# hi of w1 meets hi and lo of u in one 512-column matmul, the two halves of a PSUM bank added by VectorE

## Chip, core and metric

The kernel runs on one core of a Trainium2 chip. The metric is the device time of one execution in microseconds (us), the median of several runs. Beside it stands one profiled execution, whose trace gives every instruction's engine, start and duration.

## What is computed

Two layers of a decoder trunk on 256 tokens of width 1024, in float32. Each layer adds a token mixer and then a feed-forward part to h:

```python
for i in range(DEPTH):                       # DEPTH = 2
    u = rmsnorm(h, norm_mix[i])
    h = h + mixer_i(u)                       # i = 0: dilated window attention, i = 1: block attention
    h = h + sq_relu_mlp(rmsnorm(h, norm_ffn[i]), ffn_w1[i], ffn_w2[i])

def sq_relu_mlp(h, w1, w2):                  # w1: 1024 x 4096, w2: 4096 x 1024
    return jnp.square(jax.nn.relu(h @ w1)) @ w2
```

The change concerns `h @ w1` and the relu and square behind it.

## The kernel before

**Three matmuls for one product.** To keep float32 accuracy with matmuls that read a shorter type (F32R), each operand is split in two parts: hi, the value rounded to the shorter type, and lo, the rest. A product is then hi x hi + hi x lo + lo x hi, three matmuls that add into the same PSUM region (`mm3`, L228 to L231, and the three lines L652 to L654).

**Splitting.** Weights come from HBM in units of 256 rows by 512 columns (`next_dma`), two slices of 128 rows each. For each slice ScalarE writes hi (L165, L167) and VectorE lo (L175, L177). L167 and L177, the forms with `gt`, also multiply by the gain of the norm; the units of w1 and of the mixers' first products use them, those of w2 don't. Seven units can stand split at once.

**Order.** The program order is written by hand. Every few matmuls the code calls `beat()`: it emits the deferred steps that have come due (`defer(n, step)` means n beats from now), and on every second beat, or when the weights run short, one more slice is split. The order in which steps are emitted is the order in each engine's queue. Each engine works through its queue strictly in that order.

**u.** The normed input is transposed by TensorE (`norm_transpose`, L353). ScalarE copies it out as hi (L360) and VectorE forms lo (L361). u is two pairs of tiles (halves of four k each), one tile for hi and one for lo, 4 x 256 columns each.

**Feed-forward part** (`ffn`, L624). w1 is worked off in eight column blocks j of 512. `up(j)` forms the block's 512 hidden channels as four column blocks c of 128, with the 256 tokens as matmul columns: for each c, and for each of the eight k, three matmuls of 256 columns. `down(j)` multiplies the hidden block by w2 into two pairs of banks, with 512 columns per matmul (L229 to L231, output y). The order is up(0), up(1), down(0), up(2), down(1), and so on. In up(0) each c has a bank of its own, and the loop goes over k = 0 to 3 of all c first, since the second half of u comes later; from j = 1 on two c share one bank. The banks come from the tags "acc", "o", "s" and "tp", two of each, eight in all.

**Eviction.** `relu2` follows when a bank is full: ScalarE applies Relu out of PSUM into r (L636, one beat later), VectorE squares r (L638, three), ScalarE copies it as hi (L639, five), VectorE forms lo (L640, seven). In up(0) that is once per c with 256 columns, from j = 1 on once per two c with 512.

Of the kernel before, what the change touches and what calls it, by code (L numbers as in the profile page):

```python
# [24 lines left out]
F32 = mybir.dt.float32  # L25
F32R = mybir.dt.float32r
AF = mybir.ActivationFunctionType
ALU = mybir.AluOpType
AX = mybir.AxisListType

P = 128
S = 256
# [35 lines left out]
def trunk(ctx, tc, x, rel_bias, norm_mix, norm_ffn, a_w_qkv, a_q_gain, a_k_gain, a_w_o,  # L68
          b_w_qkv, b_q_gain, b_k_gain, b_w_o, ffn_w1, ffn_w2, onehot, mask_a, mask_b, out):
    nc = tc.nc  # L70
# [3 lines left out]
    act = ctx.enter_context(tc.tile_pool(name="act", bufs=1))  # L74
# [6 lines left out]
    def bank(tag, name):  # L81
        return ps.tile([P, 512], F32, tag=tag, bufs=2, name=name)

    def work(tag, bufs, name):
        return act.tile([P, 512], F32, tag=tag, bufs=bufs, name=name)
# [103 lines left out]
    def weight(key, k):  # L189

        i = index[key, k // 2]
        s = 2 * i + k % 2
        st["asked"] = max(st["asked"], s + 1)
        while st["hi"] <= s:
            assert next_hi(), (key, k)
        while st["lo"] <= s:
            next_lo()
        return split[i][0][:, k % 2, :], split[i][1][:, k % 2, :]

    def used(key, k):  # L200
        done.add(index[key, k // 2])
        while st["first"] in done:
            st["first"] += 1

    def defer(beats, fn):
        st["seq"] += 1
        later.append((st["beat"] + beats, st["seq"], fn))

    def beat(n=1):

        for _ in range(n):
            st["beat"] += 1
            while True:
                due = sorted(e for e in later if e[0] <= st["beat"])
                if not due:
                    break
                later.remove(due[0])
                due[0][2]()
            if st["beat"] % 2 == 0 or st["lo"] < st["asked"] + 4:
                next_slice()  # L220
# [7 lines left out]
    def mm3(acc, a, b, first, last):  # L228
        nc.tensor.matmul(acc, lhsT=a[0], rhs=b[0], start=first, stop=False)  # L229
        nc.tensor.matmul(acc, lhsT=a[0], rhs=b[1], start=False, stop=False)  # L230
        nc.tensor.matmul(acc, lhsT=a[1], rhs=b[0], start=False, stop=last)  # L231


    h = const.tile([P, NT, D], F32, name="h")
# [107 lines left out]
    u = {}  # L342
    rstd = {}

    def norm_transpose(which, half, t, natural):

        if t == 0:
            u[half] = tuple(act.tile([P, 4, S], F32R, tag=f"u{half}{s}", bufs=1, name=f"u{s}_{which}_{half}")
                            for s in ("h", "l"))
        tp = bank("tp", f"ut_{which}_{half}_{t}")  # L350
        for c in range(4):
            k = 4 * half + c
            nc.tensor.transpose(out=tp[:, c * P:(c + 1) * P], in_=h[:, t, k * P:(k + 1) * P], identity=ident)  # L353
        hi, lo = u[half]
        i = tp.rearrange("p (c q) -> p c q", c=4)
        if natural:
            hi, lo = (z.rearrange("p c (q t) -> p t c q", t=NT)[:, t] for z in (hi, lo))
        else:
            hi, lo = (z[:, :, t * P:(t + 1) * P] for z in (hi, lo))
        nc.scalar.activation(hi, i, AF.Copy)  # L360
        nc.vector.tensor_sub(lo, i, hi.bitcast(F32))  # L361
# [33 lines left out]
    def norm_half(which, half, natural=False, lead=2):  # L395
        for t in range(NT):
            defer(lead + t, lambda t=t: norm_transpose(which, half, t, natural))
        defer(lead + 3, lambda: norm_squares(which, half))
        if half == 1:
            defer(lead + 7, lambda: norm_scale(which, natural))  # L400

    def ux(k, cols):
        hi, lo = u[k // 4]
        return hi[:, k % 4, cols], lo[:, k % 4, cols]


    V, T, oT = {}, {}, {}
# [213 lines left out]
                nc.vector.scalar_tensor_tensor(hs, acc[t], scale[t], hs, op0=ALU.mult, op1=ALU.add)  # L621


    def ffn(i, after):  # L624
        hid, y = {}, {}

        def up(j):
            key = ("up", i, j)
            hh, hl = hid[j] = tuple(act.tile([P, 4, S], F32R, tag="ol", bufs=4, name=f"h{s}_{i}_{j}") for s in "hl")
            first = j == 0  # L630
            banks = {}

            def relu2(b, c0, n):
                w = n * S
                r = work("z", 3, f"r_{i}_{j}_{b}")[:, :w]
                defer(1, lambda: nc.scalar.activation(r, banks[b][:, :w], AF.Relu))  # L636
                ho, lo = (z[:, c0:c0 + n, :].rearrange("p c q -> p (c q)") for z in (hh, hl))
                defer(3, lambda: nc.vector.tensor_mul(r, r, r))  # L638
                defer(5, lambda: nc.scalar.activation(ho, r, AF.Copy))  # L639
                defer(7, lambda: nc.vector.tensor_sub(lo, r, ho.bitcast(F32)))  # L640

            for c, ks in [(c, r) for r in (range(4), range(4, 8)) for c in range(4)] if first else \
                    [(c, range(8)) for c in range(4)]:
                b, off = (c, 0) if first else (c // 2, c % 2 * S)
                if b not in banks:
                    banks[b] = bank("acc" if b < 2 else "o", f"up_{i}_{j}_{b}")
                o = banks[b][:, off:off + S]
                for k in ks:
                    whi, wlo = weight(key, k)
                    uh, ul = ux(k, slice(0, S))  # L650
                    cols = slice(c * P, (c + 1) * P)
                    nc.tensor.matmul(o, lhsT=whi[:, cols], rhs=uh, start=k == 0, stop=False)  # L652
                    nc.tensor.matmul(o, lhsT=whi[:, cols], rhs=ul, start=False, stop=False)  # L653
                    nc.tensor.matmul(o, lhsT=wlo[:, cols], rhs=uh, start=False, stop=k == 7)  # L654
                    if c == 3 and k % 2:
                        used(key, k)
                    if k % 2:
                        beat()
                if ks[-1] == 7 and first:
                    relu2(b, c, 1)  # L660
                elif ks[-1] == 7 and c % 2:
                    relu2(b, c - 1, 2)

        def down(j):
            hh, hl = hid[j]
            for n in range(2):
                key = ("down", i, j, n)
                if j == 0:
                    y[n] = [bank("so"[n], f"y_{i}_{n}_{t}") for t in range(NT)]
                tail = i == 1 and j == 7 and n == 1  # L670
                for k, t in [(k, t) for t in range(NT) for k in range(4)] if tail else \
                        [(k, t) for k in range(4) for t in range(NT)]:
                        q = slice(t * P, (t + 1) * P)
                        mm3(y[n][t], (hh[:, k, q], hl[:, k, q]), weight(key, k), j == 0 and k == 0, j == 7 and k == 3)
                        if t == 1 and k % 2:
                            used(key, k)
                        beat()
                if j == 7:
                    after(n, y[n])

        up(0)
        for j in range(8):
            if j < 7:
                up(j + 1)
            down(j)


    for t in range(NT):
        norm_transpose(0, 0, t, False)
        keep_warm(1)  # L690
        for _ in range(2):
            next_hi()
            next_lo()
    for t in range(NT):
        defer(4 + t, lambda t=t: norm_transpose(0, 1, t, False))
# [24 lines left out]
    acc = {0: [bank("acc", f"wo_a_0_{t}") for t in range(NT)]}  # L720
# [11 lines left out]
    def to_second(n, y):  # L732
        add_half(n, y, rstd)
        norm_half(2, n, natural=True, lead=3)

    ffn(0, to_second)
    place("b", lambda m: 48 + 8 * m if m < 4 else (81.5, 87.5, 94, 100.5)[m - 4],
          lambda m: 57 + 8 * m if m < 4 else 90 + 6 * (m - 4),
          lambda m: (82, 82, 88, 88, 101, 101, 113, 113)[m])
    project("b", order_b)  # L740
    acc = {0: [bank("acc", f"wo_b_0_{t}") for t in range(NT)]}
# [12 lines left out]
    def to_out(n, y):  # L754
        for t in range(NT):
            for i in range(2 if n == 1 and t == 1 else 1):
# [4 lines left out]
                (nc.scalar if i else nc.sync).dma_start(ov[:, t, c0:c0 + w], hs)  # L761

    ffn(1, to_out)
    flush()

# [26 lines left out]
```

## Time and profile before

| | |
|---|---|
| median of 3 runs | 634.81 us (634.78 to 634.92) |
| profiled execution | 634.84 us, its span 633.0 us |
| TensorE busy, matmuls | 627.3 us, 3902 instructions |
| VectorE busy | 427.1 us |
| ScalarE busy | 385.2 us |
| moved by DMA | 113.62 MB, mean 180 GB/s |

The span runs from the first to the last instruction. Busy times are unions of the instructions' durations. A matmul's duration is modelled and matmuls overlap, so what one of them costs is read from the distance of starts. Engine names in the rows: PE is TensorE, PEld its weight loads, DVE is VectorE, ACT is ScalarE, POOL is GpSimd.

### The profile page before, as it was taken

The numbers are of one execution on the slowest core, as the hardware profiler recorded it, in microseconds if no ns is written. First come the engines' busy times: TensorE is split into PE (matmuls) and PEld (weight loads), VectorE is DVE, ScalarE is ACT, GpSimd is POOL, SyncE is SP. The second block draws the span as 40 slices with busy tenths as digits, with TensorE's granted clock in tenths as the row PEclk, the third lists the DMA queues.
The fourth block names the chain that finished last, engine by engine and source line by source line (L and its number), as shares of the span: only waits on it lengthen the run. The fifth ranks groups of instructions, "written<-read, shape, count | busy, mean of one in ns | idle before, by whom it ended". The sixth has DMA issues, their size and how long they took to land.

```text
span 633.0 us, 10380 instructions
## 1 busy us (share of the span) xinstructions
PE 627.3 (99%) x3902; PEld 545.7 (86%) x3902; DVE 427.1 (67%) x767; ACT 385.2 (61%) x742; POOL 36.6 (6%) x23
## 2 busy tenths in 40 slices
PE   8999999999999999999999999999999999999997
PEld 7778887888989989998988877877999899899886
DVE  5877989766875466467547789887776744754651
ACT  6976876675765356346437778786765643653540
POOL 1222230000000000000000322000000000000000
PEclk9999999999999999999999999999999999999999
DMA  7986456423654564574556666463467446635701
GB/s 247 320 217 211 129 196 173 152 100 134 226 174 169 199 227 139 187 246 140 176 179 198 195 186 195 135 195 134 142 207 251 150 160 223 218 130 187 249 17 67
DMA packets 74538, 113.62 MB, mean 180 GB/s; under 512 B 4584, under 2 KB 30504, under 8 KB 74488
## 3 DMA queue, kind: packets, MB, share of 16 engines
q1 hardware_dynamic: 74312, 112.82, 54.6%
q8 instruction: 31, 0.51, 0.3%
q14 instruction: 19, 0.16, 0.1%
q10 hardware_dynamic: 176, 0.14, 0.1%
HBM read 111.81 MB, written 1.13 MB: 178 GB/s over the span
## 4 chain that ended last, share of the span: by engine, by line
PE 98%; DMA 1%; ACT 0%; DVE 0%; issue 0%; DVEq 0%; SPq 0%; ACTq 0%
PE up L654 10%; PE up L653 10%; PE up L652 10%; PE y L230 9%; PE y L229 9%; PE y L231 9%; PE acc_a L229 6%; PE acc_a L230 5%; PE acc_a L231 5%; PE acc_b L229 4%; PE acc_b L231 3%; PE acc_b L230 3%; PE s_a L518 1%; PE o_a L583 1%; PE ut L353 1%; PE wo_b L229 1%
## 5 line engine op out<-in xcount | busy, mean ns | idle before, releaser
L177 DVE SCALAR_TENSOR_TENSOR lo<-raw,gt,hi 128x512 fp32r<-128x512 f32 x248 | 174.5, 745 | 6.9 <-ACT hi L167 6.8
L167 ACT ACTIVATE hi<-raw,gt 128x512 fp32r<-128x512 f32 x248 | 162.9, 713 | 5.0 <-DMA raw<-in_a_w_qkv_dram 2.0
L652 PE MATMUL up<-uh,hi 128*128 128x256 f32 x512 | 145.1, 283 | 0.0
L654 PE MATMUL up<-uh,lo 128*128 128x256 f32 x512 | 144.9, 283 | 0.0
L653 PE MATMUL up<-ul,hi 128*128 128x256 f32 x512 | 144.9, 283 | 0.0
L175 DVE TENSOR_TENSOR lo<-raw,hi 128x512 fp32r<-128x512 f32 x152 | 98.3, 686 | 43.7 <-ACT hi L165 43.3
L165 ACT ACTIVATE hi<-raw 128x512 fp32r<-128x512 f32 x152 | 88.1, 624 | 54.1 <-PE up L653 21.4
L229 PE MATMUL y<-hi,hh 128*128 128x512 f32 x256 | 100.0, 390 | 0.0
L230 PE MATMUL y<-lo,hh 128*128 128x512 f32 x256 | 99.8, 390 | 0.0
L231 PE MATMUL y<-hi,hl 128*128 128x512 f32 x256 | 99.6, 389 | 0.0
L652 PEld LDWEIGHTS up<-uh,hi 128*128 128x128 f32 x512 | 98.2, 192 | 0.6
L653 PEld LDWEIGHTS up<-ul,hi 128*128 128x128 f32 x512 | 98.2, 192 | 0.5
L654 PEld LDWEIGHTS up<-uh,lo 128*128 128x128 f32 x512 | 98.2, 192 | 0.0
L638 DVE TENSOR_TENSOR r<-r 128x512 f32<-128x512 f32 (+1 forms) x36 | 22.7, 631 | 68.5 <-ACT r L636 68.5
L636 ACT ACTIVATE r<-up 128x512 f32<-128x512 f32 (+1 forms) x36 | 19.8, 550 | 76.1 <-PE up L654 75.7
L229 PE MATMUL acc_a<-hi,uh 128*128 128x512 f32 x144 | 60.3, 419 | 0.0
L231 PEld LDWEIGHTS y<-hi,hl 128*128 128x128 f32 x256 | 48.1, 188 | 10.1
L231 PE MATMUL acc_a<-hi,ul 128*128 128x512 f32 x144 | 56.7, 394 | 0.0
L230 PE MATMUL acc_a<-lo,uh 128*128 128x512 f32 x144 | 56.6, 393 | 0.0
L229 PEld LDWEIGHTS y<-hi,hh 128*128 128x128 f32 x256 | 48.1, 188 | 9.6
L230 PEld LDWEIGHTS y<-lo,hh 128*128 128x128 f32 x256 | 48.1, 188 | 9.4
L229 PE MATMUL acc_b<-hi,uh 128*128 128x512 f32 x96 | 40.0, 417 | 0.0
(128 smaller groups left out, 776.6 us busy)
## 6 DMA issues: line engine op xcount, KB each, us to landing
raw<-in_ffn_w_dram SPq DMA_DIRECT2D x128, 512.0 KB, 4.8
raw<-in_a_w_qkv_dram SPq DMA_DIRECT2D x64, 256.0 KB, 4.0
raw<-in_b_w_qkv_dram SPq DMA_DIRECT2D x24, 512.0 KB, 4.5
raw<-in_b_w_o_dram SPq DMA_DIRECT2D x8, 512.0 KB, 4.8
bias_a<-vdram_a SPq DMA_DIRECT2D x20, 128.0 KB, 5.6
raw<-in_a_w_qkv_dram SPq DMA_DIRECT2D x4, 512.0 KB, 6.3
raw<-in_a_w_o_dram SPq DMA_DIRECT2D x4, 512.0 KB
bias_b<-vdram_b SPq DMA_DIRECT2D x8, 256.0 KB, 4.6
```

Source lines behind the costliest of these rows:

```text
L165: nc.scalar.activation(hi, w, AF.Copy)
L167: nc.scalar.activation(hi, w, AF.Copy, scale=gt[:, gain + c:gain + c + 1])
L175: nc.vector.tensor_sub(lo, w, hi.bitcast(F32))
L177: nc.vector.scalar_tensor_tensor(lo, w, gt[:, gain + c:gain + c + 1], hi.bitcast(F32), op0=ALU.mult, op1=ALU.subtract)
L229: nc.tensor.matmul(acc, lhsT=a[0], rhs=b[0], start=first, stop=False)
L230: nc.tensor.matmul(acc, lhsT=a[0], rhs=b[1], start=False, stop=False)
L231: nc.tensor.matmul(acc, lhsT=a[1], rhs=b[0], start=False, stop=last)
L636: defer(1, lambda: nc.scalar.activation(r, banks[b][:, :w], AF.Relu))
L638: defer(3, lambda: nc.vector.tensor_mul(r, r, r))
L652: nc.tensor.matmul(o, lhsT=whi[:, cols], rhs=uh, start=k == 0, stop=False)
L653: nc.tensor.matmul(o, lhsT=whi[:, cols], rhs=ul, start=False, stop=False)
L654: nc.tensor.matmul(o, lhsT=wlo[:, cols], rhs=uh, start=False, stop=k == 7)
```

## The change

hi and lo of u become two planes of one tile per half, [128, 4, 2, 256], so that for each k the 256 columns of hi and the 256 of lo lie side by side. Hi of w1 then meets both in one matmul of 512 columns into a whole bank: the first half of the bank collects hi x hi, the second hi x lo. Lo of w1 meets hi of u in a matmul of 256 columns into the first half. For k = 7 the narrow matmul comes first, so that the last one covers the whole bank. Each c has a bank of its own in every up; from j = 1 on the third and fourth come from the tag "tp". VectorE adds the two halves of each bank with a `tensor_reduce` that writes 256 numbers; relu and square become one `scalar_tensor_tensor`, r = max(r, 0) x r. The steps behind are due at beats 1, 2, 4 and 6 where it was 1, 3, 5 and 7. Everything else stays.

```diff
@@ norm_transpose
-            u[half] = tuple(act.tile([P, 4, S], F32R, tag=f"u{half}{s}", bufs=1, name=f"u{s}_{which}_{half}")
-                            for s in ("h", "l"))
+            u[half] = act.tile([P, 4, 2, S], F32R, tag=f"u{half}", bufs=1, name=f"u_{which}_{half}")
...
-        hi, lo = u[half]
+        hi, lo = (u[half][:, :, s, :] for s in range(2))
@@ ux
-        hi, lo = u[k // 4]
-        return hi[:, k % 4, cols], lo[:, k % 4, cols]
+        return tuple(u[k // 4][:, k % 4, s, cols] for s in range(2))
@@ ffn, up
-            def relu2(b, c0, n):
+            def relu2(c0, n):
                 w = n * S
-                r = work("z", 3, f"r_{i}_{j}_{b}")[:, :w]
-                defer(1, lambda: nc.scalar.activation(r, banks[b][:, :w], AF.Relu))
+                r = work("z", 3, f"r_{i}_{j}_{c0}")[:, :w]
+                for c in range(c0, c0 + n):
+                    defer(1, lambda c=c: nc.vector.tensor_reduce(
+                        r[:, (c - c0) * S:(c - c0 + 1) * S], banks[c].rearrange("p (s q) -> p q s", s=2), op=ALU.add, axis=AX.X))
                 ho, lo = (z[:, c0:c0 + n, :].rearrange("p c q -> p (c q)") for z in (hh, hl))
-                defer(3, lambda: nc.vector.tensor_mul(r, r, r))
-                defer(5, lambda: nc.scalar.activation(ho, r, AF.Copy))
-                defer(7, lambda: nc.vector.tensor_sub(lo, r, ho.bitcast(F32)))
+                defer(2, lambda: nc.vector.scalar_tensor_tensor(r, r, 0.0, r, op0=ALU.max, op1=ALU.mult))
+                defer(4, lambda: nc.scalar.activation(ho, r, AF.Copy))
+                defer(6, lambda: nc.vector.tensor_sub(lo, r, ho.bitcast(F32)))
...
-                b, off = (c, 0) if first else (c // 2, c % 2 * S)
-                if b not in banks:
-                    banks[b] = bank("acc" if b < 2 else "o", f"up_{i}_{j}_{b}")
-                o = banks[b][:, off:off + S]
+                if c not in banks:
+                    banks[c] = bank("acc" if c < 2 else "o" if first else "tp", f"up_{i}_{j}_{c}")
                 for k in ks:
                     whi, wlo = weight(key, k)
-                    uh, ul = ux(k, slice(0, S))
+                    both = u[k // 4][:, k % 4].rearrange("p s q -> p (s q)")
                     cols = slice(c * P, (c + 1) * P)
-                    nc.tensor.matmul(o, lhsT=whi[:, cols], rhs=uh, start=k == 0, stop=False)
-                    nc.tensor.matmul(o, lhsT=whi[:, cols], rhs=ul, start=False, stop=False)
-                    nc.tensor.matmul(o, lhsT=wlo[:, cols], rhs=uh, start=False, stop=k == 7)
+                    if k < 7:
+                        nc.tensor.matmul(banks[c], lhsT=whi[:, cols], rhs=both, start=k == 0, stop=False)
+                    nc.tensor.matmul(banks[c][:, 0:S], lhsT=wlo[:, cols], rhs=both[:, 0:S], start=False, stop=False)
+                    if k == 7:
+                        nc.tensor.matmul(banks[c], lhsT=whi[:, cols], rhs=both, start=False, stop=True)
```

## Rows read from the trace of the kernel before

**Rows 1.** The page: engines' busy time, share, instructions; granted clock in 40 slices.
```profile
PE 627.3 (99%) x3902; PEld 545.7 (86%) x3902; DVE 427.1 (67%) x767; ACT 385.2 (61%) x742; POOL 36.6 (6%) x23
...
PEclk9999999999999999999999999999999999999999
```
**Rows 2.** The page: chain of waits that ended last, by engine and by line.
```profile
PE 98%; DMA 1%; ACT 0%; DVE 0%; issue 0%; DVEq 0%; SPq 0%; ACTq 0%
PE up L654 10%; PE up L653 10%; PE up L652 10%; PE y L230 9%; PE y L229 9%; PE y L231 9%; PE acc_a L229 6%; PE acc_a L230 5%; PE acc_a L231 5%; PE acc_b L229 4%; PE acc_b L231 3%; PE acc_b L230 3%; PE s_a L518 1%; PE o_a L583 1%; PE ut L353 1%; PE wo_b L229 1%
```
**Rows 3.** Timeline, 250 to 262 us: start, duration, engine, line, operation, operands, count.
```profile
250.41 0.39 PE L229 MATMUL y<-hi,hh 128*128 128x512 f32 x1
...
254.49 0.39 PE L229 MATMUL y<-hi,hh 128*128 128x512 f32 x1
...
255.17 0.28 PE L652 MATMUL up<-uh,hi 128*128 128x256 f32 x1
...
255.40 0.28 PE L654 MATMUL up<-uh,lo 128*128 128x256 f32 x1
...
255.52 0.28 PE L652 MATMUL up<-uh,hi 128*128 128x256 f32 x1
```
**Rows 4.** Timeline of TensorE, 262 to 268 us: the end of that up.
```profile
266.32 0.28 PE L652 MATMUL up<-uh,hi 128*128 128x256 f32 x1
...
266.68 0.40 PE L229 MATMUL y<-hi,hh 128*128 128x512 f32 x1
...
267.15 0.39 PE L231 MATMUL y<-hi,hl 128*128 128x512 f32 x1
...
267.84 0.39 PE L231 MATMUL y<-hi,hl 128*128 128x512 f32 x1
```
**Rows 5.** Instructions by line and shape: count, busy us, mean ns, idle before.
```profile
L177 DVE SCALAR_TENSOR_TENSOR lo<-raw,gt,hi 128x512 fp32r<-128x512 f32 x248 | 174.5, 745 | 6.9 <-ACT hi L167 6.8
...
L638 DVE TENSOR_TENSOR r<-r 128x512 f32<-128x512 f32 x28 | 19.4, 692 | 68.5 <-ACT r L636 68.5
...
L636 ACT ACTIVATE r<-up 128x512 f32<-128x512 f32 x28 | 16.7, 598 | 74.4 <-PE up L654 74.4
...
L537 DVE TENSOR_REDUCE nmax_a<-L_a 128x1 f32<-128x512 f32 x16 | 11.0, 686 | 0.6
L535 DVE TENSOR_TENSOR L_a<-s_a,bias_a 128x512 f32<-128x512 f32 x16 | 10.9, 683 | 1.7 <-PE s_a L518 1.6
```
**Rows 6.** Busy time by stretch: one up, one down.
```profile
255.00:266.60 11.60, 11.60 (x98) 11.56 (x97) 3.96 (x6) 3.53 (x6) 0.00 (x0) 1.00 0.49 180
266.60:277.50 10.90, 10.90 (x51) 9.04 (x50) 9.12 (x15) 8.22 (x14) 0.00 (x0) 1.00 0.56 186
```
**Rows 7.** Timeline of VectorE, 230 to 278 us: after an up.
```profile
267.51 0.69 DVE L638 TENSOR_TENSOR r<-r 128x512 f32<-128x512 f32 x1 [0.90 <-ACT r L636]
...
270.06 4.06 DVE L177 SCALAR_TENSOR_TENSOR lo<-raw,gt,hi 128x512 fp32r<-128x512 f32 x6
```
**Rows 8.** Timeline of VectorE, 140 to 186 us: first up of layer 0.
```profile
161.27 1.41 DVE L177 SCALAR_TENSOR_TENSOR lo<-raw,gt,hi 128x512 fp32r<-128x512 f32 x2
162.60 0.41 DVE L638 TENSOR_TENSOR r<-r 128x256 f32<-128x256 f32 x1
162.94 0.74 DVE L177 SCALAR_TENSOR_TENSOR lo<-raw,gt,hi 128x512 fp32r<-128x512 f32 x1
...
163.93 0.74 DVE L177 SCALAR_TENSOR_TENSOR lo<-raw,gt,hi 128x512 fp32r<-128x512 f32 x1
164.60 0.42 DVE L640 TENSOR_TENSOR hl<-r,hh 128x256 fp32r<-128x256 f32 x1
...
165.27 0.68 DVE L175 TENSOR_TENSOR lo<-raw,hi 128x512 fp32r<-128x512 f32 x1
```
**Rows 9.** Timeline of TensorE, 148 to 180 us: the second up starts.
```profile
165.48 0.28 PE L652 MATMUL up<-uh,hi 128*128 128x256 f32 x1
```

More of the change, by code (lines that the diff above doesn't have):

```diff
@@ L659, in up @@
                 if ks[-1] == 7 and first:
-                    relu2(b, c, 1)
+                    relu2(c, 1)
                 elif ks[-1] == 7 and c % 2:
-                    relu2(b, c - 1, 2)
+                    relu2(c - 1, 2)
         def down(j):
```

## The prediction, made before the changed kernel ran

> **What bounds the kernel now.** I read the engine totals first, then the chain of waits, then the matmuls one by one, and only then the other engines. TensorE has work in 627.3 of 633.0 us, its granted clock is full in every slice, and VectorE and ScalarE are busy for 67% and 61% [rows 1]. Busy TensorE alone proves little, because matmuls are pipelined. The chain of waits decides: 98% of it is TensorE, and the three matmul lines of the first feed-forward product, L652 to L654, hold 10% each [rows 2]. So whatever shortens TensorE's own sequence there shortens the kernel, as long as no other engine then comes late.
>
> How long a matmul really occupies TensorE is the distance from its start to the next start, not the duration printed beside it. In the down product (512 columns) L229 starts at 250.41 and again at 254.49 with 18 matmuls between: 4.08 / 18 = 0.2267 us each [rows 3]. In the up product (256 columns) L652 starts at 255.52 [rows 3] and, 30 groups of three later, at 266.32 [rows 4]: 10.80 / 90 = 0.1200 us each. Doubling the columns adds 0.1067 us, which is what 256 columns take at one per cycle of the 2.4 GHz level that the full clock stands for. Of either size, 0.0133 us remains that does not depend on the columns. Each matmul instruction pays it once.
>
> **The change, part by part.**
>
> *Matmuls.* A group is the work of one slice of w1 (k) on one column block (c): before, three matmuls of 256 columns, 3 x 0.1200 = 0.3600 us. After, one of 512 and one of 256 columns: 0.2267 + 0.1200 = 0.3467 us. The columns are the same 768; one fixed part goes. There are 2 layers x 8 j x 4 c x 8 k = 512 groups: 512 x 0.0133 = 6.8 us less. The weight load that goes with the removed matmul goes too; the remaining loads stand as before under the matmul ahead of them: the load for the wide one under a 256-column one, as now in every group, and the other under a longer one. That k = 7 takes lo before hi changes only the order.
>
> What the trace does not show is the two sizes alternating. It shows the changes of size. From up to down, the first two wide matmuls after the change take 0.235 us each (266.68 to 267.15) and the first five 0.232 (to 267.84), then it is 0.2267 [rows 4]. From down to up, the first two narrow ones take 0.115 (255.17 to 255.40), then it is 0.12 [rows 3]. Bounds of a group: at best 0.2267 + 0.115 = 0.3417, a saving of 512 x 0.0183 = 9.4 us; at worst 0.235 + 0.120 = 0.355, a saving of 2.6 us. In an alternation every matmul is the first after a change, so both deviations should come together, 0.232 + 0.115 = 0.347. That is the steady sum again, and I take 0.3467.
>
> The Trainium skill, page "TensorE: Matmul & The Clock Gate", section "Back-to-back issue gap", speaks against this size: an isolated warm matmul costs its columns plus 2.5 ns, so that dropping 512 of them would give 512 x 0.0025 = 1.3 us and 633.5 us. Both spacings of this trace exceed that formula by about 11 ns, and the measurement decides; a rival below keeps what is left of the rule.
>
> *Eviction.* Before, ScalarE reads a bank with Relu (L636, 0.60 us for 512 columns) and VectorE squares (L638, 0.69). After, VectorE adds the two halves of each bank with a reduce, one per c, 64 in all, and the relu and the square are one scalar_tensor_tensor. ScalarE loses its 36 Relus (28 of them on 512 columns, 16.7 us [rows 5]), which lay off the path. The reduce reads 512 numbers of a bank, in pairs 256 apart, and writes 256. No such row exists. The nearest: a reduce of 512 numbers to one, L537, 686 ns, and an add of 512 numbers out of PSUM, L535, 683 ns [rows 5]; I take 0.69 us. Bounds: 0.41 us if it ran at the pace of 256 results (L638 on 256 columns, [rows 8]), and 0.69 + (0.69 - 0.41) = 0.97 us if each result cost another step. The scalar_tensor_tensor I price like L177, 745 ns for 512 against 692 for the square [rows 5]. VectorE gains 64 x 0.69 + 36 x 0.05 = 46 us and stands at 473 of 626 us, by which it is not the bound on the mean.
>
> *Steady periods.* A period is one up and one down, 7 per layer. VectorE is busy 3.96 us of the 11.6 us of up and 9.12 us of the 10.9 us of down [rows 6]; it gains 4 x 0.69 + 2 x 0.05 = 2.9 us, 16.0 of 22.1. The burst that matters comes after an up: the square at 267.51 after 0.90 us of idle time, then the splits of w1's next block, the last six from 270.06 to 274.12 [rows 7]. The reduce of c = 2 fits into that idle time, because its bank is complete a quarter of an up earlier. The reduce of c = 3 takes the place of the Relu that VectorE waited for. So the burst moves back by 0.7 us at most (one reduce, the dearer square) to 274.8, and the next up starts 10.9 us after the last one's end at 266.6 [rows 6], at 277.5. Cost nothing; the cover is those 2.7 us. PSUM: from j = 1 on, an up holds four banks, two of the tag "acc" and two of "tp"; their reduces run at the latest just after that up, and the next up starts 10.9 us later. Cost nothing.
>
> *The first up of each layer.* Here VectorE has hardly a gap, no down lies between this up and the next, and the next up takes all eight slices of its w1 block within its first column block. In VectorE's queue the last of these splits (the last L177 ahead of the first L175) starts at 163.93 and ends at 164.67 [rows 8]. The second up starts at 165.48 [rows 9] and wants the slice for k = 7 after seven groups. In the new order three reduces come ahead of that split, and of the shorter chain one more square and the first subtraction of hl: operations follow each other some 0.08 us sooner than their durations say (two splits of 0.74 take 1.33, from 161.27 to 162.60 [rows 8]), so 3 x 0.61 + 3 x 0.05 + 0.34 + 0.34 = 2.66 us, and the split ends at 167.33. The up starts 32 x 0.0133 = 0.43 us sooner, at 165.05; the slice is wanted at 165.05 + 7 x 0.347 = 167.48, its load 0.12 us before that, at 167.36. There is no margin left. I take 0.1 us of waiting in each layer, 0.2 us; with reduces of 0.97 us it is 3 x 0.28 + 0.1 = 0.9 us in each, 1.9 us; with 0.41 us, none. TensorE waits behind the weight load alone; the rest of that up has its weights by then.
>
> *One tile for u.* hi and lo of u become two planes of one tile, so that the second half of hi (ScalarE) may have to wait for the first half of lo (VectorE), where today they are separate tiles. Taken as nothing, since TensorE has other matmuls to run during the norms; at most a part of one VectorE operation of 0.69 us, which would reach the first up as lateness and lies within its bound above.
>
> *Sum.* The profiled execution has 634.84 us, 633.0 of them span and 1.8 around it; it lies 0.03 us over the median, so that no correction is needed. 634.84 - 6.8 + 0.2 = 628.2 us.
>
> **The rivals.**
>
> *Alternating sizes eat most of the saving.* If every wide matmul behaves like the first two after a change and no narrow one gives anything back, a group takes 0.355 us: 634.84 - 2.6 + 0.2 = 632.4 us. For it: all five wide starts after an up are long. Against it: the narrow ones after a wide one are short by nearly as much.
>
> *A strained first up.* Reduces of 0.97 us and the full wait: 634.84 - 6.8 + 1.9 = 629.9 us. For it: the missing margin. Against it: both nearest rows say 0.69.
>
> *VectorE becomes the bound, and the kernel is slower.* Place: its queue in the first two ups of each layer, later every period. Each 0.1 us more per reduce costs 3 x 0.1 x 2 = 0.6 us in the first ups, so 6.6 us are gone when a reduce takes 0.69 + 1.1 = 1.8 us. In the periods VectorE's own work fills 22.0 us when four reduces take 22.0 - 13.2 = 8.8 us, 2.2 us each. At three times the row, 2.07 us, the first ups lose 3 x 1.38 x 2 + 0.2 = 8.5 us: 636.5 us. For it: stepping through a bank in pairs is nowhere in the trace. Against it: none of the operations on 512 numbers in [rows 5] takes over 0.75 us.
>
> *The product hardly gets shorter.* If the fixed 0.0133 us came not with each instruction but with each 256 columns of this type, the wide matmul would cost two narrow ones, a group would stay at 0.36 us, and the time at 634.8; if a fifth of it goes with the instruction, 1.4 us, it is 633.6 with the wait in the first ups. Against it: the down product has the same type and the double width at 0.2267, not 0.24. The skill's formula above, which knows only 2.5 ns per instruction, would end here.
>
> **How the numbers follow.** The forecast, 628.2, with its ends at 625.4 (groups of 0.3417, no wait) and 629, has 0.66; the strained first up, 629.9, 0.11; the alternation, 632.4, 0.11; the product hardly shorter, 633.6 to 634.8, 0.05; VectorE as the bound, 636.5, 0.07. The range goes from 625.4 to 632.4, the bounds of the group with those of the first ups inside; it leaves out the last two cases and a part of the alternation. A measurement of this kernel tells 0.2%, 1.3 us, from no change: faster means below 633.5. Forecast, strained first up and nearly all of the alternation are: 0.87. Within 0.2%: 0.06. Slower: 0.07.
>
> **What would show it.** Right: starts of the wide and narrow matmul that add up to 0.347 us; an up of 11.1 us where it was 11.5; reduces near 0.69 us; TensorE still nearly all of the chain. Wrong: pairs of 0.355 us; or waits of the weight load for lo in the second up of each layer well over 0.1 us; or reduces above 1 us, with VectorE in the chain during the periods.

## The result: 631.04 us, 3.8 us less

The changed kernel takes 631.04 us (median of 4 runs, 630.81 to 631.7) against 634.87 us; the ratio is 0.994, with a 95% interval of 0.9923 to 0.9958. Beside the version of the last experiment, on another chip, it was 0.9936 (0.9924 to 0.9949). The forecast was 628.2: direction and range hold, but only 3.8 of the expected 6.6 us came.

The page of the changed kernel, engines first, then the chain that ended last by engine and line, answers to [rows 1, 2]:

```profile
PE 622.7 (99%) x3390; PEld 518.0 (82%) x3390; DVE 468.5 (74%) x831; ACT 368.0 (58%) x706; POOL 36.6 (6%) x23
...
PE 96%; DVE 1%; DMA 1%; ACT 1%; issue 0%; SPq 0%; DVEq 0%; ACTq 0%
PE up L652 17%; PE up L653 10%; PE y L229 9%; PE y L231 9%; PE y L230 9%; PE acc_a L229 6%; PE acc_a L230 5%; PE acc_a L231 5%; PE acc_b L229 3%; PE acc_b L231 3%; PE acc_b L230 3%; PE up L655 2%; PE s_a L516 1%; PE o_a L581 1%; PE wo_b L229 1%; PE pt_a L559 1%
```

TensorE has 512 matmuls fewer (3902 to 3390) and still makes up nearly the whole chain. VectorE went from 427.1 to 468.5 us and does not stand in the chain for more than 1%. So the missing gain lies inside TensorE's own sequence. One up from its first matmul to the first of the down behind it, then the start of the next up, in the timeline of TensorE (start, duration, ...):

```profile
232.34 0.39 PE L652 MATMUL up<-u,hi 128*128 128x512 f32 x1
232.56 0.28 PE L653 MATMUL up<-u,lo 128*128 128x256 f32 x1
232.68 0.40 PE L652 MATMUL up<-u,hi 128*128 128x512 f32 x1
...
243.61 0.40 PE L229 MATMUL y<-hi,hh 128*128 128x512 f32 x1
...
254.50 0.39 PE L652 MATMUL up<-u,hi 128*128 128x512 f32 x1
```

243.61 - 232.34 = 11.27 us, 0.3522 us per group, where [rows 3, 4] gave 266.68 - 255.17 = 11.51 and the forecast wanted 0.3467 per group, 11.09 for the up. All steady ups agree to 0.01 us. Over them a wide matmul starts 0.235 us before the next one and a narrow one 0.117, where each in a stream of its own takes 0.2267 and 0.1200. An up and its down together, from the start of one up to the start of the next, take 254.50 - 232.34 = 22.16 us; the kernel before took 22.42 (255.17 to 277.59).

The new work of VectorE, by line and shape (count, busy us, mean ns, idle before):

```profile
L636 DVE TENSOR_REDUCE r<-up 128x256 f32<-128x512 f32 x64 | 43.7, 688 | 37.7 <-PE up L655 37.6
...
L639 DVE SCALAR_TENSOR_TENSOR r<-r 128x512 f32<-128x512 f32 x28 | 19.4, 692 | 1.0
```

The start of the profiled run differs from that of the kernel before. Two stretches of it, busy time by engine and granted clock:

```profile
5.00:8.00 3.00, 1.21 (x9) 0.92 (x7) 0.93 (x2) 1.54 (x3) 0.00 (x0) 0.97 0.90 297
8.00:15.00 7.00, 7.00 (x28) 5.34 (x29) 5.88 (x10) 6.09 (x11) 0.00 (x0) 0.77 0.87 309
```

TensorE worked 1.21 of the 3 us before 8 us, and then was granted 0.77 of its clock, a mean between its two levels of 1.2 and 2.4 GHz; before, it had worked 2.27 of the same 3 us and had the full clock throughout. What decides is not shown: in the run of the order called runs of two below it had worked 1.42 of these 3 us and kept the full clock. At the first up this run is 0.6 us later than the profile of before (153.70 against 153.11). Other runs of the same kernel have 0.999 and 1.0 of the clock over the whole span and take 0.4 us less, and the same kernel in its second profile has the full clock from 8 to 15 us and starts the first up at 152.93. So the late start belongs to the run, not to the change.

### The profile page after: what moved, and what is told of

It reads as the page before. It is cut to its first block, busy times and chain, and to the rows that moved or that the text cites. A ratio compares the mean times of both kernels' runs of the same rounds, so it can differ in the third digit from the quotient of the medians.

```text
span 629.4 us, 9371 instructions
## 1 busy us (share of the span) xinstructions
PE 622.7 (99%) x3390; PEld 518.0 (82%) x3390; DVE 468.5 (74%) x831; ACT 368.0 (58%) x706; POOL 36.6 (6%) x23
## 3 DMA queue, kind: packets, MB, share of 16 engines
HBM read 111.81 MB, written 1.13 MB: 179 GB/s over the span
## 4 chain that ended last, share of the span: by engine, by line
PE 96%; DVE 1%; DMA 1%; ACT 1%; issue 0%; SPq 0%; DVEq 0%; ACTq 0%
PE up L652 17%; PE up L653 10%; PE y L229 9%; PE y L231 9%; PE y L230 9%; PE acc_a L229 6%; PE acc_a L230 5%; PE acc_a L231 5%; PE acc_b L229 3%; PE acc_b L231 3%; PE acc_b L230 3%; PE up L655 2%; PE s_a L516 1%; PE o_a L581 1%; PE wo_b L229 1%; PE pt_a L559 1%
## 5 line engine op out<-in xcount | busy, mean ns | idle before, releaser
L177 DVE SCALAR_TENSOR_TENSOR lo<-raw,gt,hi 128x512 fp32r<-128x512 f32 x248 | 174.6, 744 | 7.4 <-ACT hi L167 7.3
L652 PE MATMUL up<-u,hi 128*128 128x512 f32 x448 | 161.1, 398 | 0.0
L653 PE MATMUL up<-u,lo 128*128 128x256 f32 x512 | 133.3, 281 | 0.0
L653 PEld LDWEIGHTS up<-u,lo 128*128 128x128 f32 x512 | 96.6, 189 | 5.9
L652 PEld LDWEIGHTS up<-u,hi 128*128 128x128 f32 x448 | 84.3, 188 | 17.8
L640 ACT ACTIVATE hh<-r 128x512 fp32r<-128x512 f32 (+1 forms) x36 | 21.1, 585 | 104.1 <-DVE r L639 104.1
L636 DVE TENSOR_REDUCE r<-up 128x256 f32<-128x512 f32 x64 | 43.7, 688 | 37.7 <-PE up L655 37.6
L229 PE MATMUL acc_a<-hi,u 128*128 128x512 f32 x144 | 60.6, 421 | 0.5 <-ACT hi L167 0.5
L231 PE MATMUL acc_a<-hi,u 128*128 128x512 f32 x144 | 57.0, 396 | 0.0
L230 PE MATMUL acc_a<-lo,u 128*128 128x512 f32 x144 | 56.9, 395 | 0.0
L229 PE MATMUL acc_b<-hi,u 128*128 128x512 f32 x96 | 40.0, 417 | 0.0
L231 PE MATMUL acc_b<-hi,u 128*128 128x512 f32 x96 | 37.6, 392 | 0.0
L230 PE MATMUL acc_b<-lo,u 128*128 128x512 f32 x96 | 37.5, 391 | 0.0
```

The lines of the kernel that those rows point to most:

```text
L177: nc.vector.scalar_tensor_tensor(lo, w, gt[:, gain + c:gain + c + 1], hi.bitcast(F32), op0=ALU.mult, op1=ALU.subtract)
L636: defer(1, lambda c=c: nc.vector.tensor_reduce(r[:, (c - c0) * S:(c - c0 + 1) * S], banks[c].rearrange("p (s q) -> p q s", s=2), op=ALU.ad ...
L640: defer(4, lambda: nc.scalar.activation(ho, r, AF.Copy))
L652: nc.tensor.matmul(banks[c], lhsT=whi[:, cols], rhs=both, start=k == 0, stop=False)
L653: nc.tensor.matmul(banks[c][:, 0:S], lhsT=wlo[:, cols], rhs=both[:, 0:S], start=False, stop=False)
```

## The experiments

Theory 1: matmuls of unlike width one behind the other take longer than their steady times add up to; each change of width costs. Theory 2: the wide matmul takes 0.235 us in this place, whatever is beside it (its operands, its bank, VectorE's reads of the neighbouring bank). Theory 3: the weight load for the wide matmul only just fits under 256 columns. Theory 4: the new eviction holds TensorE up.

**Runs of eight.** Only the order of the matmuls changes: per column block wide for k = 0 to 6, all eight narrow ones, wide for k = 7.

```diff
-                for k in ks:
-                    (wide, narrow; for k = 7 narrow, wide)
+                ops = [("w", k) for k in ks if k < 7] + [("n", k) for k in ks] + [("w", k) for k in ks if k == 7]
+                for m, (kind, k) in enumerate(ops):
+                    (that one matmul; a beat after every fourth)
```

> Per column block the wide matmuls of k = 0 to 6 stand together, then the eight narrow ones, then the wide one of k = 7: two changes of width per eight groups where there were sixteen; the same matmuls, nothing else. An up takes 11.27 us in the changed kernel, 32 groups of 0.352. Theory 1, each change of width costs about 3.3 ns: an up of 32 x 0.3467 + 4 x 0.0067 = 11.12 us, and 16 x 0.15 = 2.4 us less in all, near 628.5 us. Theory 2, the wide matmul costs 0.236 us here whatever stands beside it (operands, bank, VectorE's reads): 11.27 us as before, 631.0 us.

Its timeline, runs of like matmuls merged:

```profile
231.59 1.75 PE L655 MATMUL up<-u,hi 128*128 128x512 f32 x7
...
242.74 0.40 PE L229 MATMUL y<-hi,hh 128*128 128x512 f32 x1
...
253.64 1.07 PE L655 MATMUL up<-u,hi 128*128 128x512 f32 x4
```

11.15 us, and 629.6 us in all (629.27 to 631.26); the ratio to before is 0.9907 (0.989 to 0.9923). The same matmuls on the same operands and banks, with the same eviction, are 0.12 us faster per up when like stands beside like, and 0.11 us over up and down (22.05 against 22.16). Theory 2 falls, and with it the part of theory 4 that would slow every matmul. Theory 1 had put 11.12 us and 628.5 us: right in kind, its price of a change too small.

The kernel before shows the same delay where bank, weights and moving operand are others: its first five wide matmuls behind an up's narrow ones take 1.16 us [rows 4], and the first five wide ones behind the narrow ones inside this up take 1.16 us too, where five steady ones take 1.13.

**All 512 columns.**

```diff
-nc.tensor.matmul(banks[c][:, 0:S], lhsT=wlo[:, cols], rhs=both[:, 0:S], start=False, stop=False)
+nc.tensor.matmul(banks[c], lhsT=wlo[:, cols], rhs=both, start=False, stop=False)
```

> The narrow matmul is widened to 512 columns (lo of w1 meets hi and lo of u, a fourth product is added), so that no width changes inside an up, while operands, banks and VectorE's work stay. Theory 1: all matmuls at the steady 0.2267 us, an up of 64 x 0.2267 = 14.51 us, near 683 us in all. Theory 2: a wide matmul on u at 0.236 us, 64 x 0.2358 = 15.09 us, near 692 us.

```profile
244.88 0.39 PE L652 MATMUL up<-u,hi 128*128 128x512 f32 x1
...
259.38 0.39 PE L229 MATMUL y<-hi,hh 128*128 128x512 f32 x1
```

14.50 us for 64 matmuls, 0.2266 each; 682.63 us in all. With one width the wide matmuls on u have their steady time, in the same place with the same weights; an up and its down take 25.39 us, which is 112 x 0.2267. This speaks against theory 2 once more.

**512 and 384 columns.**

```diff
+nc.tensor.matmul(banks[c][:, 0:384], lhsT=wlo[:, cols], rhs=both[:, 0:384], start=False, stop=False)
```

> The narrow matmul is widened to 384 columns (half of the fourth product is added): the width still changes with every matmul, but a weight load has half as many columns more to hide under. Theory 1 (any change of width): 0.2267 + 0.1733 + 0.0067 = 0.4067 us per group, an up of 13.01 us, near 659 us. Theory 3, the load for the wide matmul only just fits under 256 columns and spoils the rhythm: 0.4000 us, 12.80 us, near 655.5 us. Theory 2: 0.4091 us, 13.09 us.

```profile
239.27 0.39 PE L652 MATMUL up<-u,hi 128*128 128x512 f32 x1
...
252.41 0.40 PE L229 MATMUL y<-hi,hh 128*128 128x512 f32 x1
```

13.14 us, 0.4106 per group; 661.06 us. With more room for the weight load the excess did not vanish, as theory 3 wanted; it grew, from 0.0055 us per group to 0.0106 over the steady sum of 0.2267 + 0.1733. The second of these is an estimate, halfway between the two widths; no run shows 384 columns alone, so the size of the growth is not shown. Theory 1 had forecast 13.01: right in kind, too small. Theory 3 falls by this, and by the kernel before, where every load goes under a 256-column matmul and the steady distance is 0.1200 all the same.

**Narrow matmuls, new eviction.** For k = 1 to 6 the wide matmul is split into its halves again.

```diff
+                    elif k < 7:
+                        nc.tensor.matmul(banks[c][:, 0:S], lhsT=whi[:, cols], rhs=both[:, 0:S], start=False, stop=False)
+                        nc.tensor.matmul(banks[c][:, S:], lhsT=whi[:, cols], rhs=both[:, S:], start=False, stop=False)
```

> The wide matmul of k = 1 to 6 is split into its two halves of 256 columns again; the eviction by VectorE, the banks and the one tile for u stay as in the changed kernel. 24 of 32 groups are three narrow matmuls. If the new eviction, banks or tile slow TensorE's matmuls, a narrow one takes more than 0.120 us; if not (theory 1), an up takes 24 x 0.3600 + 8 x 0.3533 = 11.47 us, and the whole 631.0 + 16 x 0.20 = 634.2 us.

```profile
233.65 0.39 PE L652 MATMUL up<-u,hi 128*128 128x512 f32 x1
...
245.04 0.40 PE L229 MATMUL y<-hi,hh 128*128 128x512 f32 x1
```

11.39 us; 634.15 us in all. Eviction, banks and the common tile do not lengthen a narrow matmul. The up is even 0.02 us under the steady sum (24 x 0.36 + 8 x 0.3467 = 11.41); the down behind it loses as much, for up and down take 22.29 us (the next up starts at 255.94), exactly the steady sum (80 x 0.12 + 56 x 0.2267). Where two wide ones stand among twenty or so narrow ones, the narrow ones give back what the wide ones take. So a change of width has no fixed price.

**The matmuls alone.** ScalarE's Relu reads the first half of each bank, as it did before; the sum of the second half is left out.

```diff
-                    defer(1, lambda c=c: nc.vector.tensor_reduce(...))
+                    defer(1, lambda c=c: nc.scalar.activation(r[:, (c - c0) * S:(c - c0 + 1) * S], banks[c][:, 0:S], AF.Relu))
```

> The matmuls, banks and tile of the changed kernel with the old eviction: ScalarE's Relu reads the first half of each bank, VectorE squares as before; the add of the second half (hi of w1 on lo of u) is left out of the result. VectorE loses its 64 reduces, 43.7 us. If the reduces are hidden everywhere: an up of 11.27 us and 631.0 us, as in the changed kernel. If they hold TensorE up, by bank or by lateness, ups get shorter: towards 11.10 us each and 628.3 us.

```profile
232.64 0.39 PE L651 MATMUL up<-u,hi 128*128 128x512 f32 x1
...
243.91 0.40 PE L229 MATMUL y<-hi,hh 128*128 128x512 f32 x1
```

11.27 us again, 23.43 and 23.41 for the first two ups of the layers together as in the changed kernel (23.43 and 23.41), 631.52 us in all in a run whose clock at the start was low (0.997 over the span). The 43.7 us of reduces are hidden everywhere. Theory 4 falls.

**Runs of two, runs of four.** How the excess depends on the number of changes. The loop of the first experiment goes over pieces of two or four k.

> Two wide matmuls, then two narrow ones: 8 changes of width per column block, against 14 in the changed kernel (k = 7 and k = 0 of the next block are both wide, k = 6 and 7 narrow side by side) and 2 in runs of eight. Without any cost of changes an up is 32 x 0.3467 = 11.09 us; the changed kernel has 0.177 us more over 56 changes, 3.2 ns each; the runs of eight 0.06 us over 8, 7.5 ns each. If a change costs a fixed 3.2 ns: 11.20 us. If a change upsets the matmuls behind it until some five of a kind have run, so that it costs more the longer the run: near 11.25 us, hardly better than alternating. In all 630 to 631 us.

> Four wide, then four narrow: 4 changes per column block, 16 per up. A fixed 3.2 ns per change: 11.14 us. A cost that grows with the run, about 7 ns at this length: 11.20 us. In all 629 to 630.5 us.

```profile
231.52 0.62 PE L655 MATMUL up<-u,hi 128*128 128x512 f32 x2
...
242.75 0.40 PE L229 MATMUL y<-hi,hh 128*128 128x512 f32 x1
```

```profile
231.50 1.07 PE L655 MATMUL up<-u,hi 128*128 128x512 f32 x4
...
242.68 0.40 PE L229 MATMUL y<-hi,hh 128*128 128x512 f32 x1
```

| order, 32 wide and 32 narrow | changes per up | up, us | over 11.09 | up and down, us | over 21.97 | per change |
|---|---|---|---|---|---|---|
| alternating (changed kernel) | 56 | 11.27 | 0.18 | 22.16 | 0.19 | 3.3 ns |
| runs of two | 32 | 11.23 | 0.14 | 22.13 | 0.15 | 5 ns |
| runs of four | 16 | 11.18 | 0.09 | 22.07 | 0.09 | 6 ns |
| runs of eight | 8 | 11.15 | 0.06 | 22.05 | 0.08 | 10 ns |

(The count: for k = 7 the narrow one comes first, so two narrow ones meet inside a column block and two wide ones at its border; alternating has 14 changes per block, not the 16 of the first expectation.) The price per change is worked out from up and down together, with a steady sum of 32 x 0.3467 + 48 x 0.2267 = 21.97 us, because part of what the last change of an up costs falls into the down: the up alone would give 7 ns for runs of eight. The kernel before, with two changes in an up and its down, has 22.42 us where its steady sum is 22.40, again 10 ns per change. The fewer the changes, the shorter the up, in every step. A fixed price is refuted, since it would have given 11.20 and 11.14; a price that grows with the run had been put at 11.25 and 11.20. Both measured values lie between. In all 631.91 us and 629.34 us, one run each; the first is above its forecast because 3.7 us of it lie outside the span of 628.2 us, where about 2 are usual. Why is not shown.

**Each reduce twice.**

```diff
-                for c in range(c0, c0 + n):
+                for c in [c for c in range(c0, c0 + n) for _ in range(2)]:
```

> Each reduce is issued twice, so VectorE has 64 more of 0.69 us. In the first up of each layer three more come ahead of the split that the second up wants for k = 7: it ends 3 x 0.61 = 1.8 us later. In the changed kernel it ends at 167.93 us and is wanted near 168.2, so the margin is 0.3 us and TensorE should wait 1.5 us per layer in the second up: 634 us, all other ups 11.27 us. If the steady periods have no room either, their ups get longer as well, by up to 1.2 us each, towards 650 us. If nothing is late: 631.0 us.

In the second up of layer 0 the split for k = 7 (timeline of VectorE) and the narrow matmuls for k = 6 and 7 (of TensorE):

```profile
169.43 0.74 DVE L177 SCALAR_TENSOR_TENSOR lo<-raw,gt,hi 128x512 fp32r<-128x512 f32 x1
```

```profile
168.28 0.28 PE L653 MATMUL up<-u,lo 128*128 128x256 f32 x1
170.23 0.38 PE L653 MATMUL up<-u,lo 128*128 128x256 f32 x1 [1.68 <-DVE lo L177]
```

The waits of TensorE list the same line twice, once per layer:

```profile
PE up L653 <- DVE lo L177: 3.4, 2, 1.7
```

The matmul for k = 7 starts 1.95 us after its neighbour instead of 0.12, 1.83 us lost, and the first two ups of a layer take 25.30 us instead of 23.43. The expectation had 1.5: a doubled reduce starts 0.72 us behind its twin and not 0.61, three of them are 2.16 us, and the margin of 0.27 us is all that covers it. All other ups keep their 11.27. The place that the prediction named is the only one that gives. In all 636.22 us against an expected 634: the span is 633.3 us, 3.9 more than in the profile of the changed kernel, of which 2 x 1.87 are the loss in the first two ups; the other 2.9 us lie outside the span, where that profile had 1.8.

**The two versions side by side.**

> The changed kernel once more, beside the next one on the same chip, so that both are compared with the same runs of the kernel before. Ups of 11.27 us; 3.8 to 4.0 us less than before, a ratio near 0.994.

> The runs of eight once more. Its ups of 11.15 us are 0.117 us shorter than those of the changed kernel, twelve of them, and 0.2 us in the first two ups of each layer: 12 x 0.117 + 2 x 0.2 = 1.8 us less, a ratio near 0.991. If the order of the matmuls were no cause, both would have the same time.

Against the same runs of the kernel before: the changed kernel 630.85 us, 0.9936 (0.9924 to 0.9949); runs of eight 629.62 us, 0.9909 (0.9894 to 0.9924). Ups of 11.27 and 11.15 us as before. The medians are 1.2 us apart where up and down explain 1.7 (12 x 0.107 + 2 x 0.2). The runs of one kernel scatter by more than that gap, 630.75 to 632.7 and 628.95 to 630.14, but the two ranges do not touch: the version with runs beats both others.

## Why the prediction was right or wrong

**The bound.** Right: TensorE's sequence sets the end before and after, and what was saved there came out in the time: 512 x (0.3600 - 0.3522) = 4.0 us, with 3.8 measured.

**The fixed part of a matmul.** Right, as far as one width goes: 0.2266 us in an up of 512-column matmuls only, the value of the down product in [rows 3]. The formula of the Trainium skill ("TensorE: Matmul & The Clock Gate", section "Back-to-back issue gap"), which the page gives for an isolated matmul, would have 0.2158 with its 2.5 ns per instruction. No run here shows that, and the measurement decides.

**The step that failed** is the one behind "in an alternation every matmul is the first after a change, so both deviations should come together, 0.232 + 0.115 = 0.347". Both came, but not with equal weight: wide ones 0.235, narrow ones 0.117, together 0.3522. The term was mis-sized by 512 x 0.0055 = 2.8 us. 628.2 + 2.8, less the 0.2 of waiting that did not come, is 630.8, and that is what the runs of the changed kernel with nearly the full clock took (630.81 and 630.84). The bounds were right (0.3417 to 0.355); the fault was to take the sum of two transients, each read off a single place (0.115 is half of 0.23 us, printed to 0.01), as a proof that they cancel. The steady value had no more standing than the two ends, and the middle of the bounds, 0.3484, would have been no better founded but nearer. The rival with the alternation had the mechanism, at 632.4 as its end; the truth lies between it and the forecast, nearer to the rival.

**The eviction.** Right: 688 ns for the reduce against 0.69 taken, 468.5 us of VectorE against 473. The scalar_tensor_tensor took 692 ns and not 745: it costs what the square did, and the dearer L177, which also reads a factor for each partition, was the wrong neighbour. No consequence.

**Steady periods.** Right, and the cover is there: doubling all reduces left them at 11.27.

**One tile for u.** Right, nothing is to be seen: in the first up of layer 0 the first eight groups take 3.60 us to the start of the ninth (153.70 to 157.30), before 3.66 (153.11 to 156.77).

**The first up of each layer.** The place was right, and the time of the split was right. The rows of the changed kernel (VectorE, then TensorE), which answer to [rows 8, 9]:

```profile
167.19 0.74 DVE L177 SCALAR_TENSOR_TENSOR lo<-raw,gt,hi 128x512 fp32r<-128x512 f32 x1
```

```profile
167.97 0.40 PE L652 MATMUL up<-u,hi 128*128 128x512 f32 x1
168.20 0.40 PE L653 MATMUL up<-u,lo 128*128 128x256 f32 x2
168.44 0.40 PE L655 MATMUL up<-u,hi 128*128 128x512 f32 x1
```

The split ends at 167.93; less the 0.6 us by which this run is later from its start, that is 167.35, and the forecast was 167.33. Its matmul is the second of the two at 168.20, whose load goes under the first: a margin of 0.27 us where none was expected. The slower pairs made most of it, 39 groups up to there by 0.0055 us, 0.21 us. So the 0.2 us of waiting in the sum did not come, and not because the working was right: the error in the groups gave the margin. At the forecast pace the wait might have come.

**The rivals.** VectorE as the bound is out by the 688 ns; with the reduces doubled, the loss was 1.83 us per layer in the one place named, and the span came out as long as that of the kernel before (633.3 against 633.0 us). The strained first up is out by the same 688 ns and the missing wait. A product that hardly gets shorter is out by the all-512 run, with 0.2266 us for a wide matmul and not 0.24.

## What to carry to other kernels

Fewer, wider matmuls save a fixed cost per instruction, here 13 ns each, but 2.8 of the 6.8 us were lost again because wide and narrow ones alternated; put like widths side by side, and the order alone brings about half of that back. Where a trace shows a new pattern only by its two transitions, keep their bounds and do not let them cancel on paper. Work that moves to an engine with time to spare is free in the steady loop, but look for the one place without a gap, here two column-block products in a row, and work out its margin there.

## What was not expected of the hardware

A sequence of matmuls of 512 and 256 columns takes up to 0.0055 us per pair more than the two take in streams of their own, with 512 and 384 about 0.0106, if 384 columns alone take 0.1733. The excess falls with the number of changes but not in proportion: 3.3 ns per change when alternating, about 10 in runs of eight and between up and down of the kernel before, none over an up and its down where two wide ones stand among many narrow ones. It does not come from the weight load having too little room (with 384 columns the load has more room and the excess stays), nor from VectorE (the same 11.27 us without the reduces), nor from the banks and operands alone (the same ones in runs of eight lose less than half). What makes it is open: no run here looks inside the engine.
